# Later modulation steps tied to the end of a weight chunk, the last remainders and pooling sums on one engine, transposes in longer rows

## The chip, the cores and the metric

The kernel runs on one core of one Trainium2 chip. The metric is the device time of one execution in microseconds (us), as the median of several runs; a profiled execution gives the rows of the trace. The profile names the engines PE (TensorE, the matmuls), PEld (its weight loads), DVE (VectorE), ACT (ScalarE), POOL (GpSimd) and SP (SyncE, which here issues the loads of the weights).

## The reference

One decoder layer for 256 new prompt tokens and 8 sequences of 4 new tokens each, so 288 columns in all. Both get the same weights; `c` is a conditioning vector for each sequence.

```python
def decoder_layer(x, c, s0, conv_buf, pool_buf, pos0, w_ada, b_ada, norm1_g, w_in, ..., w_down):
    mod = jax.nn.silu(c) @ w_ada + b_ada
    sh1, sc1, gt1, sh2, sc2, gt2 = jnp.split(mod, 6, axis=-1)
    u = ada_modulate(rms_norm(x, norm1_g), sh1, sc1)
    mix, s_new, conv_new, pool_new = token_mixers(u, conv_buf, s0, pool_buf, pos0, w_in, conv_w, ...)
    x = x + gt1[:, None, :] * mix
    h = ada_modulate(rms_norm(x, norm2_g), sh2, sc2)
    gate, up = jnp.split(h @ w_gate_up, 2, axis=-1)
    x = x + gt2[:, None, :] * ((jax.nn.silu(gate) * up) @ w_down)
    return x, s_new, conv_new, pool_new

def token_mixers(u, ...):
    proj = u @ w_in                        # 2048 -> 9232: q, k, v, z, a, b, xpool, ga, gb
    qkv, conv_new = causal_conv_silu(jnp.concatenate([q, k, v], axis=-1), conv_buf, conv_w)
    ...                                    # gated delta rule over chunks of 64 tokens
    y_p, pool_new = multiscale_pool(xpool, pool_buf, pos0)   # window sums over 2, 4, 8, 16 tokens
    merged = jax.nn.sigmoid(ga) * y_a + jax.nn.sigmoid(gb) * y_b
    return merged @ w_out, s_new, conv_new, pool_new
```

## The kernel before

Every large product goes through `gemm` (L127): a panel of 512 output channels by 288 columns in four PSUM tiles `g` of 128 channels. To keep float32 accuracy, each weight is split into a rounded high part `wh` and a low remainder `wl`, and each 128x128 block is multiplied three times (wh by the high and by the low part of the input, wl by the high part). Weights come in chunks of two blocks of 128 rows: 512 KB, loaded by `load_raw` (L104) through SP's queue into a ring `raw` of 7 slots, cast to `wh` by ACT (L123) and subtracted to `wl` (L124) by DVE or, where `gemm` is told so, by POOL. Four tiles each of `wh` and `wl` hold two chunks. A chunk is 24 matmuls, all on L141.

At the end of each chunk `gemm` calls `fill()` (L146). It counts `every` up and, at each whole number, steps a generator that lays the modulation's products in between: `ada` (L181). A step takes four 512 KB pieces of `w_ada` through the same ring and runs 8 matmuls (L218, tile `ada`; 16 records in the trace); after eight steps four transposes (L225) and an addition (L231) finish 2048 of the modulation's channels. `first_ada` gives those that are needed at once. Three later groups, `later` (M_GT1, M_SC2, M_SH2), are stepped every fifth chunk from the last step of the first product on; `last_ada` (M_GT2) is stepped through the output product and the feed-forward part, with its first two steps' loads ahead.

The first product runs over nine panels (FIRST: q, pooling input, k, pooling input, v, z and three gate panels) in five STEPS of the contraction, so each panel is added into `acc` by DVE at each step after the first (L435). In the last step, four of the nine panels (the odd ones) have their remainders `wl` made by POOL instead of DVE. In that same stretch of time, from about 255 to 345 us, the causal convolution runs on DVE (`conv_evac`, L286, L289, L292), with small copies on POOL (L275 to L281). The pooling branch makes window sums by doubling (`win`, L893): the first of each pair of channel blocks on POOL, the second on DVE; then `yp` (L896 to L900) on DVE.

Three other places transpose on PE: `conv_state_out` (L822, rows of four); the residual input `x` ahead of each of the four panels of the output product (L1011; its tile `xr` takes a slot of a pool of two and is loaded by a DMA that POOL issues, L1008); and `turn` (L1125, tile `pf`) at the end of each panel of the down product.

The tile framework's scheduler puts the instructions of each engine into one order. `tc.high_priority()` makes what is inside go as early as it may, and `tc.issue_after(ins)` puts an instruction behind another one of the same engine in that order.

## Time and profile before

| | |
|---|---|
| median of three runs | 1805.72 us (1804.52 to 1808.49) |
| profiled execution | 1801.66 us |
| its span, first to last instruction | 1799.8 us |
| mean granted TensorE clock | 0.995 |
| PE busy | 1749.2 us, 97% of the span |
| DVE busy | 1001.3 us, 56% |
| ACT busy | 751.0 us, 42% |
| POOL busy | 234.0 us, 13% |

The profiled execution is 1.86 us longer than its span; it lies 4.06 us below the median of the three runs and 2.86 us below the fastest of them. Busy times are means over the whole program; single stretches differ much.

### The profile page before, as it was taken

To read this page: it belongs to the slowest core of one execution; us is meant where nothing else is said; L and a number is where in the kernel's file an instruction comes from. 1 tells how busy PE (TensorE), PEld (TensorE's weight loads), DVE (VectorE), ACT (ScalarE), POOL (GpSimd) and SP (SyncE) were. 2 spreads that over 40 slices of the span, in tenths; PEclk is the share of its full clock that TensorE was granted. 3 is DMA by queue.
4 is the path that set the end of the run, shared out by engine and by line. 5 is a ranking of instruction groups with operands and counts; after the bars stand their busy time and mean duration, and the time that the engine had idled before them with its cause. 6 is when DMAs were issued, how large, how long until landed. Compare 5 with 4: busy or idle time off the path is not lost.

```text
span 1799.8 us, 37784 instructions
## 1 busy us (share of the span) xinstructions
PE 1749.2 (97%) x14772; PEld 1651.6 (92%) x14772; DVE 1001.3 (56%) x2101; ACT 751.0 (42%) x1534; POOL 234.0 (13%) x391
## 2 busy tenths in 40 slices
PE   5999998999999999999999999999999999999997
PEld 3979997888899898899989999999999999999997
DVE  2456569755666676764564444455445445544454
ACT  4523346542344333444444444444334444444333
POOL 1000015420222444211241000000000000000000
PEclk9999999999999999999999999999999999999999
DMA  9988756677577585885647667665555555555542
GB/s 292 316 300 304 234 169 202 213 229 246 187 252 234 189 268 177 271 294 179 218 150 234 211 205 224 188 203 165 164 165 164 168 167 169 154 175 164 162 156 87
DMA packets 227210, 371.23 MB, mean 206 GB/s; under 512 B 18335, under 2 KB 118168, under 8 KB 226608
## 3 DMA queue, kind: packets, MB, share of 16 engines
q1 hardware_dynamic: 223224, 357.02, 61.7%
q0 software_dynamic: 3808, 11.80, 2.1%
q8 instruction: 116, 1.90, 0.4%
q14 instruction: 62, 0.51, 0.1%
HBM read 361.16 MB, written 7.96 MB: 205 GB/s over the span
## 4 chain that ended last, share of the span: by engine, by line
PE 91%; DMA 4%; DVE 2%; issue 1%; ACT 0%; POOL 0%; SPq 0%; DVEq 0%; POOLq 0%; ACTq 0%
PE g L141 81%; PE ada L218 4%; DMA raw<-in_w_ada_dram 3%; DVE wl L124 1%; PE pks L726 1%; DVE cy L286 0%; DMA raw<-in_w_in_dram 0%; PE py L646 0%; PE pp L651 0%; PE pnr L545 0%; PE py L907 0%; DMA xt<-in_x_prompt_dram 0%; PE px L1011 0%; DMA pw<-in_pool_w_dram 0%; DMA dtb<-in_dt_bias_dram 0%
## 5 line engine op out<-in xcount | busy, mean ns | idle before, releaser
L141 PE MATMUL g<-rq,wh 128*128 128x288 f32 x7296 | 1443.2, 298 | 10.6 <-DVE acc L435 6.2
L141 PEld LDWEIGHTS g<-rq,wh 128*128 128x128 f32 x7296 | 1150.8, 188 | 37.2 <-issue 10.9
L141 PE MATMUL g<-rq,wl 128*128 128x288 f32 x3648 | 1014.3, 296 | 0.3 <-POOL wl L124 0.3
L124 DVE TENSOR_TENSOR wl<-raw,wh 128x512 fp32r<-128x512 f32 x910 | 611.7, 702 | 627.0 <-ACT wh L123 606.7
L123 ACT CAST wh<-raw 128x512 fp32r<-128x512 f32 x944 | 545.3, 618 | 821.7 <-PE g L141 742.5
L141 PEld LDWEIGHTS g<-rq,wl 128*128 128x128 f32 x3648 | 664.8, 188 | 4.3 <-issue 1.3
L218 PE MATMUL ada<-raw,cpad 128*32 128x512 f32 (+2 forms) x1152 | 98.5, 474 | 16.0 <-DMA raw<-in_w_ada_dram 16.0
L169 POOL TENSOR_TENSOR ro<-ro,cfix 128x1 f32<-128x1 f32 (+1 forms) x3 | 1.6, 559 | 838.0 <-DVE ro L1150 838.0
L218 PEld LDWEIGHTS ada<-raw,cpad 128*32 128x32 f32 x1152 | 32.9, 115 | 52.8 <-issue 38.1
L435 DVE TENSOR_TENSOR acc<-acc,g 128x288 f32<-128x288 f32 x144 | 61.0, 448 | 23.3 <-PE g L141 23.0
L124 POOL TENSOR_TENSOR wl<-raw,wh 128x512 fp32r<-128x512 f32 x34 | 45.8, 1367 | 51.6 <-ACT wh L123 50.4
L141 PE MATMUL g<-q,wh 128*128 128x288 f32 x256 | 49.4, 294 | 0.0
L286 DVE SCALAR_TENSOR_TENSOR cy<-xc,vb,cy 128x312 f32<-128x312 f32 x72 | 42.5, 610 | 5.6 <-ACT cy L284 4.7
L141 PEld LDWEIGHTS g<-q,wh 128*128 128x128 f32 x256 | 40.3, 189 | 0.0
L141 PE MATMUL g<-q,wl 128*128 128x288 f32 x128 | 35.2, 296 | 0.0
L1099 DVE SCALAR_TENSOR_TENSOR fgg<-fth,fgg 128x288 f32<-128x288 f32 x44 | 20.0, 455 | 14.0 <-ACT fgg L1098 14.0
L973 DVE SCALAR_TENSOR_TENSOR x<-g,mod,x 128x256 f32<-128x256 f32 x48 | 22.9, 478 | 7.0 <-PE g L141 5.9
L1097 ACT ACTIVATE fth<-g 128x288 f32<-128x288 f32 x44 | 18.3, 416 | 13.5 <-PE g L141 13.4
L141 PEld LDWEIGHTS g<-q,wl 128*128 128x128 f32 x128 | 23.2, 188 | 0.0
L659 POOL MEMSET T<- 32x64 f32 x8 | 1.1, 155 | 156.7 <-PE pab L444 148.4
L1104 DVE TENSOR_TENSOR fgg<-fgg,g 128x288 f32<-128x288 f32 x44 | 19.9, 451 | 2.7 <-PE g L141 0.4
L1098 ACT ACTIVATE fgg<-g 128x288 f32<-128x288 f32 x44 | 18.4, 417 | 0.0
(336 smaller groups left out, 976.2 us busy)
## 6 DMA issues: line engine op xcount, KB each, us to landing
raw<-in_w_gate_up_dram SPq DMA_DIRECT2D x352, 256.0 KB, 2.9
raw<-in_w_in_dram SPq DMA_DIRECT2D x144, 512.0 KB, 4.6
raw<-in_w_ada_dram SPq DMA_DIRECT2D x128, 512.0 KB, 5.6
raw<-in_w_down_dram SPq DMA_DIRECT2D x88, 512.0 KB, 4.0
raw<-in_w_ada_dram SPq DMA_DIRECT2D x128, 256.0 KB, 5.5
raw<-in_w_out_dram SPq DMA_DIRECT2D x32, 512.0 KB, 3.9
raw<-in_w_proj_b_dram SPq DMA_DIRECT2D x16, 512.0 KB, 4.5
raw<-in_w_proj_a_dram SPq DMA_DIRECT2D x16, 512.0 KB, 4.6
```

The lines of the kernel that those rows point to most:

```text
L123: act.copy(wh[i], raw[:, i, :])
L124: eng.tensor_tensor(wl[i], raw[:, i, :], wh[i].bitcast(F32), ALU.subtract)
L141: mm = pe.matmul(o, w[i][:, j * P:(j + 1) * P], xs(kbs[c + i])[x], start=c + n == 0, stop=last and n == 3 * KB - 1)
L218: in_turn(pe.matmul(ps[32 * j:32 * j + 32, 0:w], cpad[:, k + i, :], raws[x][:, i, q * w:(q + 1) * w], start=c == 0 and y < 4, stop=c + ste ...
L286: vec.scalar_tensor_tensor(y[:, 0:L], xc[:, m:m + L], vb[:, 24 * m + no:24 * m + no + 1], y[:, 0:L], ALU.mult, ALU.add)
L435: vec.tensor_tensor(a, a, ps, ALU.add)
L726: pe.matmul(pks[NS * i:NS * i + NS, x * P:(x + 1) * P], km[i // 2][:, i % 2, b, :], S[i][:, b, :], start=b == 0, stop=b == NB - 1)
L973: vec.scalar_tensor_tensor(x[:, j, 0:NP], ps[:, 0:NP], mod[:, gate + d, 0:1], x[:, j, 0:NP], ALU.mult, ALU.add)
L1097: act.activation(th, ps, AF.Tanh, scale=0.5)
L1098: act.activation(gg, ps, AF.Copy, scale=0.5)
L1099: vec.scalar_tensor_tensor(gg, th, 1.0, gg, ALU.add, ALU.mult)
L1104: vec.tensor_tensor(gg, gg, ps, ALU.mult)
```

## The change

After each chunk, `gemm` keeps its last matmul in `fill.last`. A step of a late modulation group (16 tiles of output at once, `m == 16`, and not loaded ahead) now stops once more between its loads and its matmuls, and its first matmul is put behind the last matmul of the chunk that was just written out; so a step takes two calls, and `every` is doubled to keep the pace (0.2 to 0.4, and 0.085 to 0.17). In the last step of the first product all `wl` are on DVE, and so are all window sums. The transposes of `conv_state_out`, of `x` and of `turn` are written out together, with the later ones at high priority, and the samples' piece of `xr` takes a slot of the ring `raw`.

```diff
@@ -143,6 +143,7 @@
                 if last:
                     with tc.high_priority():
                         evac(j, o)
+            fill.last = mm
             fill()
         return mm
 
@@ -210,11 +211,14 @@
             yield
         for c in range(0, 16, step * pair):
             loads = early.get(c) or load(c, pool)
+            tied = m == 16 and c not in early
+            if tied:
+                yield
 
             todo = [(k, raws, i, j) for k, raws in reversed(loads) for i in range(step) for j in (2, 3, 0, 1)]
             for y, (k, raws, i, j) in enumerate(todo):
                 x, q = divmod(j, 4 // per)
-                with tc.high_priority() if y else nullcontext():
+                with tc.high_priority() if y else tc.issue_after(fill.last.ins) if tied else nullcontext():
                     in_turn(pe.matmul(ps[32 * j:32 * j + 32, 0:w], cpad[:, k + i, :], raws[x][:, i, q * w:(q + 1) * w],
                                       start=c == 0 and y < 4, stop=c + step * pair == 16 and y + 4 >= len(todo)))
             if c + step * pair < 16:
@@ -241,7 +245,7 @@
 
     class Fill:
 
-        gen, every, n = iter(()), 1.0, 0.0
+        gen, every, n, last = iter(()), 1.0, 0.0, None
 
         def __call__(self):
             self.n += self.every
@@ -425,7 +429,7 @@
 
             more = n + 1 < len(STEPS)
             fill.gen = first_ada(*STEPS[n + 1], st) if more else later
-            fill.every = 4 / (dn // KB * len(FIRST) - 5) if more else 0.2
+            fill.every = 4 / (dn // KB * len(FIRST) - 5) if more else 0.4
             for p, c0 in enumerate(FIRST):
                 def evac(j, ps, n=n, p=p):
                     a = acc[p][:, j, :]
@@ -433,7 +437,7 @@
                         act.copy(a, ps)
                     else:
                         vec.tensor_tensor(a, a, ps, ALU.add)
-                gemm(cols_of(w_in, c0), parts(uh, ul), evac, range(k0, k1), gp if n + p == 0 or not more and p % 2 else vec)
+                gemm(cols_of(w_in, c0), parts(uh, ul), evac, range(k0, k1), gp if n + p == 0 else vec)
                 if p == 1:
                     if n == 0:
                         wab = st.tile([P, 16, 32], F32, name="wab")
@@ -820,11 +824,15 @@
             vec.tensor_tensor(zv, hv(pot), zv, ALU.mult)
 
     def conv_state_out():
+        pls = []
         for p in range(6):
             c0 = 512 * p
-            pl2 = aux("plc")
-            for j in range(4):
-                pe.transpose(pl2[0:27, j * P:(j + 1) * P], cbd[:, 4 * p + j, :], ident)
+            if p % 3 == 0:
+                pls = [aux("plc", i) for i in range(3)]
+                for j in range(12):
+                    with tc.high_priority() if j else nullcontext():
+                        pe.transpose(pls[j // 4][0:27, j % 4 * P:(j % 4 + 1) * P], cbd[:, 4 * p + j, :], ident)
+            pl2 = pls[p % 3]
             ltok = wide("lct")[0:27].rearrange("p h n -> p (h n)")
             act.copy(ltok, pl2[0:27, :])
             dmg(out=t["new_conv_prompt"][0, 0, :, c0:c0 + 512], in_=ltok[0:3, :])
@@ -890,7 +898,7 @@
                     while have < w:
                         nx = pl.tile([P, POOLW], F32, tag="win", name="win", bufs=3)
                         lo = 2 * have - 1
-                        (vec if j else gp).tensor_tensor(nx[:, lo:], s[:, lo:], s[:, lo - have:POOLW - have], ALU.add)
+                        vec.tensor_tensor(nx[:, lo:], s[:, lo:], s[:, lo - have:POOLW - have], ALU.add)
                         s, have = nx, 2 * have
                     yp = pl.tile([P, N], F32, tag="yp", name="yp", bufs=2)
                     vec.scalar_tensor_tensor(yp[:, 0:NP], s[:, 15:XPW], 1.0 / w, src[:, 15:XPW],
@@ -1002,14 +1010,19 @@
     for p in range(4):
         x = fquad(f"x{p}")
         xq.append(x)
+        xrs = []
         for i, (src, n) in enumerate(((t["x_prompt"][0, 0:P], P), (t["x_prompt"][0, P:2 * P], P),
                                       (t["x_sample"].rearrange("b s d -> (b s) d"), NS))):
-            xr = wide("xr")[0:n].rearrange("p h n -> p (h n)")
+            xr = wide("xr").rearrange("p h n -> p (h n)") if i < 2 else load_raw([], kbs=1)[0:n, 0, 0:512]
             dmg(out=xr, in_=src[:, 512 * p:512 * p + 512])
-            px = aux("px")
-            for d in range(4):
-                pe.transpose(px[:, d * n:(d + 1) * n], xr[:, d * P:(d + 1) * P], ident[0:n, 0:n])
-            act.copy(x[:, :, i * P:i * P + n], px[:, 0:4 * n].rearrange("p (d n) -> p d n", n=n))
+            xrs.append((xr, n))
+        pxs = [aux("px", i) for i in range(3)]
+        for y, (i, d) in enumerate((i, d) for i in (2, 1, 0) for d in range(4)):
+            xr, n = xrs[i]
+            with tc.high_priority() if y else nullcontext():
+                pe.transpose(pxs[i][:, d * n:(d + 1) * n], xr[:, d * P:(d + 1) * P], ident[0:n, 0:n])
+        for i, (xr, n) in enumerate(xrs):
+            act.copy(x[:, :, i * P:i * P + n], pxs[i][:, 0:4 * n].rearrange("p (d n) -> p d n", n=n))
 
         def evac(j, ps, p=p, x=x):
             add_gated(x, j, 4 * p + j, ps, M_GT1)
@@ -1037,7 +1050,7 @@
         mm = gemm(cols_of(t["w_out"][0], 512 * p), xs_m, evac, range(16))
     with tc.issue_after(mm.ins):
         next(last_ada)
-    fill.every, fill.n = 0.085, 0
+    fill.every, fill.n = 0.17, 0
 
 
     rn = cst.tile([P, 3], F32, name="rn")
@@ -1123,9 +1136,11 @@
             pfs = [aux("pf", i) for i in range(3)]
 
             def turn(d0, d1, m, p=p, pfs=pfs):
+                for y, (d, i) in enumerate((d, i) for d in reversed(range(d0, d1)) for i in (2, 1, 0)):
+                    t0, n = toks[i]
+                    with tc.high_priority() if y else nullcontext():
+                        pe.transpose(pfs[i][0:n, d * P:(d + 1) * P], xq[p][:, d, t0:t0 + n], ident)
                 for i, (t0, n) in enumerate(toks):
-                    for d in range(d0, d1):
-                        pe.transpose(pfs[i][0:n, d * P:(d + 1) * P], xq[p][:, d, t0:t0 + n], ident)
                     jf = ff.tile([P, 512], F32, tag="jf", name="jf", bufs=2)
                     w = slice(d0 * P, d1 * P)
                     act.activation(jf[0:n, w], pfs[i][0:n, w], AF.Square, accum_out=sso[0:n, i, m:m + 1])
```

What that does to the order of the instructions shows at three places. A row has its number, the line, the operation, the tiles and the shape; in the changed file lines after 146 are 1 to 15 higher. The first place is DVE in the last step of the first product, around the additions into acc_255, the third panel (k). Before:

```order
239 L124 TENSOR_TENSOR wl<-raw,wh 128x512
240 L896 SCALAR_TENSOR_TENSOR yp<-win,xp 128x256
241 L289 SCALAR_TENSOR_TENSOR acc_253<-cth,cy 128x256
242 L292 SCALAR_TENSOR_TENSOR smp<-cth,cy 128x32
243 L900 SCALAR_TENSOR_TENSOR yp<-win,xp 128x32
244 L286 SCALAR_TENSOR_TENSOR cy<-xc,vb,cy 128x312
245 L898 TENSOR_TENSOR yp<-win,icnt 128x15 x2
246 L435 TENSOR_TENSOR acc_255<-acc_255,g_3219 128x288
247 L435 TENSOR_TENSOR acc_255<-acc_255,g_3220 128x288
248 L435 TENSOR_TENSOR acc_255<-acc_255,g_3221 128x288
249 L435 TENSOR_TENSOR acc_255<-acc_255,g_3222 128x288
250 L899 TENSOR_TENSOR yp<-yp,xp 128x15 x2
```

And after:

```order
242 L124 TENSOR_TENSOR wl<-raw,wh 128x512
243 L904 SCALAR_TENSOR_TENSOR yp<-win,xp 128x256
244 L908 SCALAR_TENSOR_TENSOR yp<-win,xp 128x32
245 L124 TENSOR_TENSOR wl<-raw,wh 128x512
246 L290 SCALAR_TENSOR_TENSOR cy<-xc,vb,cy 128x312 x2
247 L906 TENSOR_TENSOR yp<-win,icnt 128x15
248 L439 TENSOR_TENSOR acc_255<-acc_255,g_3228 128x288
249 L439 TENSOR_TENSOR acc_255<-acc_255,g_3229 128x288
250 L906 TENSOR_TENSOR yp<-win,icnt 128x15
251 L439 TENSOR_TENSOR acc_255<-acc_255,g_3230 128x288
252 L439 TENSOR_TENSOR acc_255<-acc_255,g_3231 128x288
```

Before, one `wl` and a run of pooling and convolution rows stand directly ahead of the four additions; after, the `wl` of more chunks (row 245, and row 254 behind) stand here, the sums L901 that fed `yp` have moved ahead of this piece, and the convolution's L293 and L296 of acc_253 have gone behind the additions. POOL's order loses 16 rows of L124 and 10 of L893 over the whole program; DVE's gains them.

The second place is PE in the later panels of w_in, where a modulation step stood 56 matmuls of `g` behind the one before it. Before (row 1895 is the step):

```order
1889 L141 MATMUL g_6391<-rq,wl 128x288
1890 L618 MATMUL pgm<-smp 128x128
1891 L141 MATMUL g_6388<-rq,wh 128x288 x2
1892 L141 MATMUL g_6389<-rq,wh 128x288 x2
1893 L141 MATMUL g_6390<-rq,wh 128x288 x2
1894 L141 MATMUL g_6391<-rq,wh 128x288 x2
1895 L218 MATMUL ada<-raw,cpad 32x512 x8
1896 L141 MATMUL g_6388<-rq,wl 128x288
1897 L141 MATMUL g_6388<-rq,wh 128x288 x2
1898 L141 MATMUL g_6389<-rq,wl 128x288
```

And after, the step that stands nearest to it, at the end of a chunk (g_6388 begins the next panel):

```order
1868 L141 MATMUL g_6017<-rq,wl 128x288
1869 L141 MATMUL g_6018<-rq,wh 128x288 x2
1870 L141 MATMUL g_6018<-rq,wl 128x288
1871 L141 MATMUL g_6018<-rq,wh 128x288 x2
1872 L141 MATMUL g_6018<-rq,wl 128x288
1873 L222 MATMUL ada<-raw,cpad 32x512 x8
1874 L760 MATMUL po<-w,at 128x128 x4
1875 L141 MATMUL g_6388<-rq,wh 128x288 x2
1876 L141 MATMUL g_6388<-rq,wl 128x288
```

Before, the 8 matmuls of a step stood inside a chunk, many of them at distances of 54 to 205 matmuls of `g` from the step before; after, they stand directly behind a chunk, 114 to 126 matmuls of `g` apart. SP's queue keeps its pattern of four pieces of w_ada and five chunks of weights. Counted along both orders, the last three pieces of a step and the first chunk behind them now mostly wait for slots that the step before sets free, and that chunk's first matmul stands 66 to 72 matmuls of `g` behind that step (96 and more for most chunks before).

The third place is PE at the end of the first panel of the down product, where `pf` is made. Before, the first rows of it:

```order
7638 L1128 MATMUL pf<-cfix,x_10696 128x128 x2
7639 L141 MATMUL g_20892<-rq,wh 128x288 x2
7640 L141 MATMUL g_20892<-rq,wl 128x288
7641 L141 MATMUL g_20892<-rq,wh 128x288 x2
7642 L141 MATMUL g_20892<-rq,wl 128x288
7643 L1128 MATMUL pf<-cfix,x_10696 32x128
7644 L1128 MATMUL pf<-cfix,x_10696 128x128 x2
7645 L141 MATMUL g_20891<-rq,wh 128x288 x2
7646 L141 MATMUL g_20892<-rq,wh 128x288
7647 L1128 MATMUL pf<-cfix,x_10696 32x128
7648 L141 MATMUL g_20893<-rq,wh 128x288 x2
```

And after:

```order
7644 L141 MATMUL g_20893<-rq,wh 128x288 x2
7645 L1142 MATMUL pf<-cfix,x_10696 128x128 x8
7646 L141 MATMUL g_20894<-rq,wh 128x288 x2
7647 L141 MATMUL g_20894<-rq,wl 128x288
7648 L141 MATMUL g_20894<-rq,wh 128x288 x2
7649 L141 MATMUL g_20894<-rq,wl 128x288
7650 L1142 MATMUL pf<-cfix,x_10696 32x128 x4
7651 L141 MATMUL g_20891<-rq,wl 128x288
```

The twelve transposes stood in seven rows of one to three among the next panel's matmuls; now they stand in one of eight and one of four. In the order of the x transposes (L1011) the rows stay at four, but those of panels 1 to 3 stand 37 to 51 matmuls of `g` behind the ones that set their slot of `xr` free.

## Rows read from the trace of the kernel before

**Rows 1.** The profile's page: busy time, share of the span, instructions.

```profile
PE 1749.2 (97%) x14772; PEld 1651.6 (92%) x14772; DVE 1001.3 (56%) x2101; ACT 751.0 (42%) x1534; POOL 234.0 (13%) x391
```

**Rows 2.** The chain that ended last: lines' shares; pieces (start, us, what).

```profile
PE g L141 81%; PE ada L218 4%; DMA raw<-in_w_ada_dram 3%; DVE wl L124 1%; PE pks L726 1%; DVE cy L286 0%; DMA raw<-in_w_in_dram 0%; PE py L646 0%; PE pp L651 0%; PE pnr L545 0%; PE py L907 0%; DMA xt<-in_x_prompt_dram 0%; PE px L1011 0%; DMA pw<-in_pool_w_dram 0%; DMA dtb<-in_dt_bias_dram 0%
...
1172.16 506.58 PE g L141 x3816
```

**Rows 3.** What PE waited for, 255 to 345 us: total, times, longest.

```profile
PE g L141 <- DVE acc L435: 5.8, 4, 4.4
...
PE g L141 <- POOL wl L124: 0.3, 1, 0.3
```

**Rows 4.** Timeline of PE: start, us, what, idle before and its releaser.

```profile
284.68 0.50 PE L141 MATMUL g<-rq,wh 128*128 128x288 f32 x2 [4.37 <-DVE acc L435]
```

**Rows 5.** Timeline of DVE around that wait.

```profile
275.59 0.68 DVE L124 TENSOR_TENSOR wl<-raw,wh 128x512 fp32r<-128x512 f32 x1
276.20 0.53 DVE L286 SCALAR_TENSOR_TENSOR cy<-xc,vb,cy 128x312 f32<-128x312 f32 x1
...
280.79 1.48 DVE L289 SCALAR_TENSOR_TENSOR acc<-cth,cy 128x256 f32<-128x256 f32 x1
282.20 1.25 DVE L292 SCALAR_TENSOR_TENSOR smp<-cth,cy 128x32 f32<-128x32 f32 x1
...
286.45 0.58 DVE L893 TENSOR_TENSOR win<-xp 128x422 f32<-128x422 f32 x1
286.95 0.41 DVE L289 SCALAR_TENSOR_TENSOR acc<-cth,cy 128x256 f32<-128x256 f32 x1
287.29 0.21 DVE L292 SCALAR_TENSOR_TENSOR smp<-cth,cy 128x32 f32<-128x32 f32 x1
```

**Rows 6.** Timeline of POOL around it.

```profile
278.76 4.63 POOL L124 TENSOR_TENSOR wl<-raw,wh 128x512 fp32r<-128x512 f32 x3
```

**Rows 7.** Windows: us, busy of PE, PEld, DVE, ACT, POOL, then PEclk, DMA share, GB/s.

```profile
262.00:290.00 28.00, 22.52 (x156) 20.26 (x156) 26.56 (x51) 15.74 (x43) 20.90 (x38) 0.94 0.59 189
285.00:290.00 5.00, 5.00 (x29) 5.00 (x28) 4.93 (x12) 2.65 (x8) 4.02 (x8) 0.66 0.37 111
...
255.00:345.00 90.00, 83.23 (x642) 74.31 (x644) 76.35 (x170) 51.95 (x124) 47.25 (x88) 0.98 0.65 209
```

**Rows 8.** Groups of instructions, 255 to 380 us: count, busy us, mean ns.

```profile
L124 POOL TENSOR_TENSOR wl<-raw,wh 128x512 fp32r<-128x512 f32 x16 | 21.9, 1389 | 19.0 <-ACT wh L123 19.0
L893 POOL TENSOR_TENSOR win<-win 128x420 f32<-128x420 f32 (+2 forms) x6 | 6.9, 1154 | 1.8 <-DVE yp L898 1.5
...
L893 POOL TENSOR_TENSOR win<-xp 128x422 f32<-128x422 f32 x4 | 4.5, 1113 | 10.8 <-ACT xp L859 10.7
```

**Rows 9.** DVE's convolution group, 255 to 345 us.

```profile
L286 DVE SCALAR_TENSOR_TENSOR cy<-xc,vb,cy 128x312 f32<-128x312 f32 x36 | 23.4, 664 | 0.7 <-POOL cbd L280 0.4
```

**Rows 10.** The same group, 345 to 1799 us.

```profile
L286 DVE SCALAR_TENSOR_TENSOR cy<-xc,vb,cy 128x312 f32<-128x312 f32 x36 | 19.2, 556 | 4.9 <-ACT cy L284 4.7
```

**Rows 11.** What PE waited for, 200 to 1799 us.

```profile
PE ada L218 <- DMA raw<-in_w_ada_dram: 1.2, 2, 0.8
```

**Rows 12.** Chain that ended last, from 480 us.

```profile
490.72 9.31 DMA raw<-in_w_ada_dram
...
500.08 1.92 PE ada L218 x16
```

**Rows 13.** Timeline of SP, 480 to 505 us.

```profile
489.27 1.95 SPq L114 DMA_DIRECT2D raw<-in_w_ada_dram  x4
```

**Rows 14.** DMA issues, 480 to 1168 us: count, KB each, median us to landing.

```profile
raw<-in_w_ada_dram SPq DMA_DIRECT2D x88, 512.0 KB, 6.1
```

**Rows 15.** Tile xr (span of the run).

```profile
DMA to landing us min/median/max: 2.2/3.8/6.3
```

**Rows 16.** Chain that ended last, from 834 us.

```profile
839.76 0.44 PE px L1011 x4
```

**Rows 17.** Chain that ended last, from 1715 us.

```profile
1718.34 0.22 PE pf L1128 x2
```

## The prediction, made before the changed kernel ran

> **What bounds the kernel now.** I began with the page: PE is busy for 97% of the span [rows 1]. The chain of work that ended last says the same in another way: 81% of the span is the matmuls of `g`, and its longest piece is 3816 of them in 506.58 us without a gap [rows 2]. That gives the pace of this kernel, 506.58/3816 = 0.13275 us for a matmul, about 3.2 us for a chunk of 24. The number of these matmuls does not change, so the change can only give or take the time in which PE stands still, runs slowly or does something else. I therefore read what PE waited for. In the stretch from 255 to 345 us, which is the last step of the first product, PE waited four times for DVE's additions L435, 5.8 us in all, and once for POOL's `wl`, 0.3 us [rows 3]. One of the four waits is nearly all of it: 4.37 us before 284.68 [rows 4].
>
> Why DVE was late there is seen on its own timeline. The multiply-add L289 takes 0.41 us at 286.95 and took 1.48 us at 280.79; L292 takes 0.21 us and took 1.25 us [rows 5]. In the same microseconds POOL ran three `wl` in a row, from 278.76 to 283.39 [rows 6]. DVE was busy for 26.56 us of the 28 us from 262 to 290 [rows 7]: it was full, and it was full partly of slowed instructions. PE paid twice. After the wait the granted clock was lower for a while: 0.66 as a mean over 285 to 290 us, so partly at the lower of its two levels, 1.2 instead of 2.4 GHz, with 29 matmuls in 5.00 us [rows 7], where 29 x 0.13275 = 3.85 us would do. That is 1.15 us more, and it follows on a stretch in which the engine had stood still for 4.37 us.
>
> **The remainders and the sums on DVE.** Removed from POOL are 16 `wl` of 1389 ns, 21.9 us, and ten sums, 6.9 + 4.5 = 11.4 us [rows 8]. DVE gets them at its own price. The pitch from one start to the next is the honest one, since neighbouring instructions overlap a little: 276.20 - 275.59 = 0.61 us for a `wl` and 286.95 - 286.45 = 0.50 us for a sum [rows 5]. So DVE gains 16 x 0.61 + 10 x 0.50 = 14.8 us of work. What it gets back is the slowing. The 36 multiply-adds L286 in the stretch took 664 ns each [rows 9], the other 36, later, 556 [rows 10]: 36 x 0.108 = 3.9 us. L289 and L292 lost 1.07 and 1.04 us in one place alone [rows 5]. So at least 6.0 us come back on rows that I can price, and at most the 33.3 us of POOL's work. The rest of the 14.8 us must fit into DVE's pauses, which are 90.00 - 76.35 = 13.65 us from 255 to 345 us [rows 7], and it does fit on the whole: 14.8 - 6.0 = 8.8.
>
> Whether it fits at the one place that counts is read from the order. Between the additions to the second and the third panel, DVE now has four `wl`, five L290, three sums, four short `yp` and little else. At 0.61, 0.53 (L286 at 276.20 [rows 5]), 0.50 and some 0.3 us that is 2.4 + 2.7 + 1.5 + 1.2 = 7.8 us, and the four additions follow. PE has 86 matmuls between the same points, 86 x 0.13275 = 11.4 us. So the additions should be ready in time, and the wait of 4.37 us goes, with the 1.15 us of slow clock behind it: **-5.5 us**. The other end on the good side is that every wait of the stretch goes, 5.8 + 0.3 + 1.15 = -7.3. The other end on the bad side is that the wait stays, 0, or that DVE, which has 28.00 - 26.56 = 1.44 us to spare there, becomes later by what the moved `wl` cost; 8 of the 16 and 3 sums stood there, 6.4 us against 1.44 of pause and at least 2.1 of slowing, so +2.9 at worst. I take the middle of the three, since the new order puts the convolution's L293 and L296 behind the additions.
>
> **The tied steps.** They cost no matmul and no load. PE waited twice for a piece of w_ada after 200 us, 1.2 us in all [rows 11]. One of them is in the chain that ended last: the piece took 9.31 us and the step's 16 records began at 500.08 [rows 12]. Its matmuls stood only a few chunks behind the load's issue at 490.72, and the load took 9.31. With 114 to 126 matmuls (15.1 to 16.7 us) between steps that is covered: **-1.2 us**. The other end is 0.
>
> The price stands in the queue behind the step. Three pieces and then one chunk of weights now go out on the slots which a step sets free, and the chunk is wanted 66 to 72 matmuls later. A step takes 1.92 us [rows 12]; the first slot is free some 0.5 us into it, and the chunk must have landed one cast (0.6 us) ahead of its matmul. So it has 1.92 + 72 x 0.13275 - 0.6 = 10.9 us from the step's start. If it lands as most pieces do, 6.1 us after its issue [rows 14], it is there at 1.9 + 6.1 = 8.0 us, and nothing is lost. If it fares as the four pieces that SP issued from 489.27 on [rows 13], the last of which landed at 490.72 + 9.31 = 500.03 [rows 12], four take 10.8 us, and it is there at 0.5 + 10.8 = 11.3 us, 0.4 late with 72 matmuls and 1.2 late with 66. The 24 late steps at some 0.5 us make **0 to +12 us**. I take +1.5, three steps that meet other traffic, because the median piece is 2.9 us early and the one case of 10.8 us was the worst that PE's waits show.
>
> **The transposes.** A row of four on `x` is 0.44 us of the chain [rows 16] and a row of two on `pf` 0.22 [rows 17], so 0.11 us each, in short rows as in long ones. Longer rows neither save nor cost: **0** (0.1 either way). The samples' `xr` no longer takes a slot of the pool of two, so POOL's loads start earlier. But the order puts the prompt's transposes of three panels 37 to 51 matmuls, 4.9 to 6.8 us, behind the release of their slot, and such a load lands after 2.2 to 6.3 us, 3.8 in the middle [rows 15]. Mostly it is there. At worst four rows wait 6.3 - 4.9 = 1.4 us each: 0 to +5.6; I take **+0.7**. The conv state's rows move 24 transposes of unchanged price.
>
> **The sum.** -5.5 - 1.2 + 1.5 + 0 + 0.7 = -4.5 us against the profiled execution, 1801.66 - 4.5 = 1797.2. That execution lies 4.06 us below the median of the three runs, and I add that back: **1801.2 us**. Within 0.2% of 1805.72, that is 3.6 us or 1802.1 to 1809.3, a measurement of this kernel can hardly tell from no change; the forecast lies only just outside.
>
> **The rivals.**
>
> *DVE stays late.* For it speaks that DVE had 1.44 us to spare in the 28 us and gets 6.4 us of work there; against it that the order gives it less ahead of the additions. Then the wait shrinks only by the slowing less the three `wl` that ran beside it, 2.1 - 3 x 0.61 = 0.3 us, and the slow clock stays: -0.3 - 1.2 + 1.5 + 0.7 = +0.7, **1806.4**, the same.
>
> *POOL held DVE for all of its time.* Then DVE gets back much more than the 6 us that I priced, and all the small waits go too: -7.3 instead of -5.5, **1799.4**. The trace has only the slowed rows in POOL's time for it [rows 5, 6], and against it that L286 lost only 108 ns in the mean [rows 9, 10]. The Trainium skill (SBUF — State Buffer, Who interferes with whom) states a rule for this: the two engines share a pair of ports as an exclusive lock, and the loser blocks fully. The trace agrees where L289 and L292 take 1.48 and 1.25 us, but the 36 L286 lost 3.9 us beside POOL's 33.3 us of work, so the lock did not bite all the time. The Trainium skill (Perfetto Trace Analysis, Optimizing Scalar/DVE Operations) says that moving work off a saturated DVE to GpSimd might not help for that reason, which speaks for taking such work back; no run here shows that yet.
>
> *Weights late behind the pieces of w_ada.* For it: the one group of four that a wait shows took 10.8 us. Against it: the median of 6.1. It decides where the chunk lands later than 10.9 us after a step's start. Without the +1.5 the sum is -6.0; 24 steps of 0.5 make it +6.0: 1801.66 + 6.0 + 4.06 = **1811.7**, slower.
>
> *The x transposes wait for their loads.* With +5.6 instead of +0.7 the sum is +0.4: **1806.1**, the same. That the change does not do what it says is not a rival: both orders are there to be read.
>
> **How the numbers follow.** My forecast has 0.41, POOL's full hold 0.14, late DVE 0.25, late weights 0.13, the x transposes 0.07. Faster: all of the full hold and four fifths of the forecast's case, which lies at the bound, 0.14 + 0.33 = 0.47. Slower: the late weights and a few hundredths of late DVE at its worst end (+2.9 with late transposes), 0.16. The rest is the same, 0.37. The likeliest case alone reaches from 1799 to 1803.5. The range goes down to the full hold with the best of the unknown terms (1799.4 - 2.2 - 1.2 = 1796.0) and up to the late DVE at its worst (1806.4 + 2.9 = 1809.3); beyond it lie late weights and little else.
>
> **What would show it.** In the changed profile, PE should wait for L439 in the stretch at most half a microsecond at a time, and no slow clock should follow at 285 us; L290 should take some 560 ns and L293 some 0.4 us there, and DVE should be busy above 85% from 255 to 345 us. No wait for w_ada should be left after 200 us. If weights come late, PE waits for ACT's cast, which waits for raw<-in_w_in or w_proj, once every five chunks. If the loads of `xr` come late, PE waits for them at 820 to 860 us. The prediction is wrong if the wait before the third panel's next matmuls is still above 2 us, or if such waits for casts add up to more than 3 us.

## The result, and the profile after

The changed kernel takes 1814.94 us in the median of five runs (1813.29 to 1815.53), the kernel before 1805.65 in the five beside them: ratio 1.0058, 95% interval 1.0047 to 1.0070. It is slower by 9.3 us, outside the range and on the other side of the forecast. The profiled execution has a span of 1813.2 us against 1799.8 before; some 4 of these 13.4 us are not the change's, since the execution traced before lies 4.06 us below its median.

What was meant to happen to the waits of the first stretch did happen. The waits of PE in the changed kernel, from 255 to 345 us and then from 150 to 1790 (total, times, longest):

```profile
PE pnr L549 <- ACT sq L546: 1.5, 1, 1.5
PE g L141 <- ACT wh L123: 0.9, 2, 0.5
PE g L141 <- DVE smp L296: 0.7, 1, 0.7
...
PE pot L818 <- DVE oo L815: 4.8, 1, 4.8
PE g L141 <- ACT wh L123: 3.2, 6, 0.9
PE g L141 <- ACT rq L1083: 2.3, 1, 2.3
PE g L141 <- DVE ga L967: 2.2, 1, 2.2
```

The waits for DVE's additions, 5.8 us before [rows 3], are gone from the stretch, and no wait for w_ada is left there or later [rows 11]. In their place stand a wait of `pnr` for ACT, six waits for casts (two of them in the stretch), a wait of `pot` for DVE and one of `g` for DVE's `ga`. (The 2.3 us for `rq` are old.) DVE in the stretch, as a window (us, busy of PE, PEld, DVE, ACT, POOL, then granted clock, DMA share, GB/s) and as groups (count, busy us, mean ns):

```profile
255.00:345.00 90.00, 86.84 (x687) 79.06 (x685) 75.79 (x195) 55.10 (x132) 28.56 (x69) 0.96 0.60 196
```

```profile
L124 DVE TENSOR_TENSOR wl<-raw,wh 128x512 fp32r<-128x512 f32 x41 | 27.6, 685 | 7.1 <-ACT wh L123 7.0
L290 DVE SCALAR_TENSOR_TENSOR cy<-xc,vb,cy 128x312 f32<-128x312 f32 x36 | 18.5, 536 | 0.8 <-ACT cy L288 0.7
...
L293 DVE SCALAR_TENSOR_TENSOR acc<-cth,cy 128x256 f32<-128x256 f32 x12 | 5.0, 417 | 0.1
```

Two of these groups before:

```profile
L124 DVE TENSOR_TENSOR wl<-raw,wh 128x512 fp32r<-128x512 f32 x24 | 17.4, 736 | 5.7 <-ACT wh L123 5.2 <-POOL cbd L281 0.5
L289 DVE SCALAR_TENSOR_TENSOR acc<-cth,cy 128x256 f32<-128x256 f32 x12 | 6.7, 561 | 0.3
```

DVE's busy time is 75.79 us where it was 76.35 [rows 7], though it makes 41 `wl` where it made 24: the multiply-adds fell from 664 ns [rows 9] to 536, and what POOL does fell from 47.25 to 28.56 us. What the moved work costs DVE came back from instructions that take less time when POOL does less beside them. The runs below bear this out: the multiply-adds take 538 ns in `b_dve`, which moves this work alone, and 679 in `n_nodve`, which leaves it on POOL. The Trainium skill (Perfetto Trace Analysis, Optimizing Scalar/DVE Operations) says that moving operations between GpSimd and DVE might not help. The trace agrees: with 16 remainders and ten sums taken back, DVE is busy for 997.7 us of the whole program, where it was 1001.3.

Three places show where the time went. First, the wait of `pnr`. The timelines of SP, then of ACT (start, us, what, idle before and its releaser):

```profile
271.88 3.87 SPq L114 DMA_DIRECT2D raw<-in_w_ada_dram  x4
275.79 9.58 SPq L114 DMA_DIRECT2D raw<-in_w_in_dram  x4
```

```profile
285.22 0.62 ACT L123 CAST wh<-raw 128x512 fp32r<-128x512 f32 x1 [1.16 <-DMA raw<-in_w_in_dram]
285.75 1.14 ACT L546 ACTIVATE sq<-acc 128x512 f32<-128x512 f32 x2
```

Four pieces of w_ada went out, and chunks of w_in right behind them. The chain of work of this stretch names one of these loads:

```profile
276.92 8.22 DMA raw<-in_w_in_dram
```

ACT stood before the cast of that chunk, and `sq`, which stands behind the cast on ACT, was what PE waited for. Second, the wait for `ga`, on ACT, DVE and PE:

```profile
800.39 1.14 ACT L123 CAST wh<-raw 128x512 fp32r<-128x512 f32 x2 [6.06 <-DMA raw<-in_w_proj_a_dram]
```

```profile
801.04 0.69 DVE L124 TENSOR_TENSOR wl<-raw,wh 128x512 fp32r<-128x512 f32 x1 [5.92 <-ACT wh L123]
801.65 0.81 DVE L967 SCALAR_TENSOR_TENSOR ga<-ga,g 128x288 f32<-128x288 f32 x2
```

```profile
802.24 0.50 PE L141 MATMUL g<-rq,wh 128*128 128x288 f32 x2 [2.22 <-DVE ga L967]
```

The timeline of SP and the chain of work name the chunk:

```profile
788.98 2.51 SPq L114 DMA_DIRECT2D raw<-in_w_ada_dram  x4
791.59 11.87 SPq L114 DMA_DIRECT2D raw<-in_w_proj_a_dram  x4
```

```profile
791.59 8.70 DMA raw<-in_w_proj_a_dram
```

Here too the chunk directly behind four pieces is late, and what PE waited for is the instruction queued behind its remainder. Third, the longest wait, on POOL and PE:

```profile
651.63 0.89 POOL L945 DMA_DIRECT2D sst<-in_state_delta_dram  x1 [7.07 <-DMA out_dram<-sst]
652.54 0.72 POOL L170 TENSOR_TENSOR m<-m,cfix 128x2 f32<-128x2 f32 x1
```

```profile
655.46 0.66 PE L818 MATMUL pot<-cfix,oo 128*128 128x128 f32 x2 [4.82 <-DVE oo L815]
```

POOL waits 7.07 us for the store of a delta state before it can issue the next reload into that buffer; the small reciprocal root `m`, on which DVE's `oo` and then PE's `pot` wait, stands behind it in POOL's order. Before, the second root stood ahead of the reload next to it, and that reload waited for 0.77 us:

```profile
648.41 0.73 POOL L169 TENSOR_TENSOR m<-m,cfix 128x2 f32<-128x2 f32 x1 [1.33 <-DVE m L808]
649.12 1.29 POOL L780 TENSOR_TENSOR wx<-wr,cm 96x512 fp32r<-96x512 f32 x1
651.17 0.95 POOL L937 DMA_DIRECT2D sst<-in_state_delta_dram  x1 [0.77 <-DMA out_dram<-sst]
```

After each of the three waits the granted clock was lower, partly at 1.2 instead of 2.4 GHz, in windows of 8, 8 and 5 us:

```profile
287.00:295.00 8.00, 8.00 (x41) 8.00 (x41) 6.44 (x16) 3.72 (x11) 1.30 (x8) 0.57 0.33 108
655.00:663.00 8.00, 7.54 (x44) 7.55 (x45) 5.87 (x14) 2.02 (x5) 1.36 (x3) 0.69 0.76 216
802.00:807.00 5.00, 4.76 (x24) 4.79 (x25) 5.00 (x13) 2.10 (x5) 0.53 (x1) 0.66 0.36 110
```

The slower running is the larger part of the loss. The page of the changed kernel has, for the same 14772 instructions [rows 1]:

```profile
PE 1759.5 (97%) x14772; PEld 1658.2 (91%) x14772; DVE 997.7 (55%) x2127; ACT 751.5 (41%) x1534; POOL 205.3 (11%) x365
```

PE is busy for 10.3 us more (1759.5 against 1749.2) and idle for 3.1 us more (span less busy time, 53.7 against 50.6): of the 13.4 us between the two spans, three quarters are PE being busy for longer with the same instructions, and the rest is standing still. The mean granted clock is 0.990, and was 0.995.

### The profile page after: what moved, and what is told of

Its sections match the earlier page's. It is cut to its first block, busy times and chain, and to the rows that moved or that the text cites. A ratio compares the mean times of both kernels' runs of the same rounds, so it can differ in the third digit from the quotient of the medians.

```text
span 1813.2 us, 37744 instructions
## 1 busy us (share of the span) xinstructions
PE 1759.5 (97%) x14772; PEld 1658.2 (91%) x14772; DVE 997.7 (55%) x2127; ACT 751.5 (41%) x1534; POOL 205.3 (11%) x365
## 4 chain that ended last, share of the span: by engine, by line
PE 91%; DMA 6%; DVE 1%; ACT 1%; issue 1%; POOL 0%; SPq 0%; DVEq 0%; ACTq 0%; POOLq 0%
PE g L141 80%; PE ada L222 4%; DMA raw<-in_w_in_dram 1%; DMA raw<-in_w_ada_dram 1%; DMA out_dram<-sst 1%; DMA raw<-in_w_proj_b_dram 1%; PE pks L730 1%; PE py L915 0%; DMA raw<-in_w_proj_a_dram 0%; PE py L650 0%; DVE wl L124 0%; PE pp L655 0%; PE pnr L549 0%; ACT wh L123 0%; DMA xt<-in_x_prompt_dram 0%
## 5 line engine op out<-in xcount | busy, mean ns | idle before, releaser
L124 DVE TENSOR_TENSOR wl<-raw,wh 128x512 fp32r<-128x512 f32 x926 | 618.0, 696 | 636.5 <-ACT wh L123 617.3
L124 POOL TENSOR_TENSOR wl<-raw,wh 128x512 fp32r<-128x512 f32 x18 | 23.9, 1349 | 33.9 <-ACT wh L123 32.8
```

The costliest lines, as they stand in the source:

```text
L124: eng.tensor_tensor(wl[i], raw[:, i, :], wh[i].bitcast(F32), ALU.subtract)
```

## The experiments

The ratios below are those of the runs against runs of the kernel before beside them on the same chip; a difference between two versions is one of medians, which for most pairs were not measured side by side. A trace shows one execution only, and those of `b_tied`, `a_near` and `a_near_root` are the shortest of their runs (1811.70, 1799.70 and 1800.08 us). Theory A says that the tied steps are the loss. Within it, A1 names POOL's order and A2 late weights. Theories B (the longer rows and the ring slot of `xr`) and C (a full DVE) are its rivals.

**Each part alone, and the change without its tied steps.** `b_tied` is the kernel before with the lines of `ada`, `fill.last` and `every` alone; its core:

```diff
+            tied = m == 16 and c not in early
+            if tied:
+                yield
...
-                with tc.high_priority() if y else nullcontext():
+                with tc.high_priority() if y else tc.issue_after(fill.last.ins) if tied else nullcontext():
```

> The kernel before with only the tied modulation steps (and the doubled pace). Theory A (the tied steps are the loss: they move the chunk boundaries, weights come late behind three pieces of w_ada, and POOL's queue puts a reciprocal root behind a state load that waits): the whole loss and the gain of the other parts is missing, so +10 to +16 us against before, with a wait of PE's pot for DVE's oo of 4 to 5 us near 650 us. Theory B (the loss is in the rows: the x transposes and the ring slots taken by the samples' xr): within 3 us of before.

1817.08 us, ratio 1.0063 (1.0042 to 1.0085): the whole loss, as theory A has it. PE's waits for `pot` and for casts, of the sort seen above, are there with this part alone, the one of `pot` shorter than the 4 to 5 us that theory A wanted:

```profile
PE g L141 <- ACT wh L123: 3.0, 4, 1.4
PE pot L818 <- DVE oo L815: 3.0, 1, 3.0
```

`b_dve` takes the `gemm(..., gp if n + p == 0 else vec)` and the `vec` window sums alone.

```diff
-                gemm(..., range(k0, k1), gp if n + p == 0 or not more and p % 2 else vec)
+                gemm(..., range(k0, k1), gp if n + p == 0 else vec)
-                        (vec if j else gp).tensor_tensor(nx[:, lo:], ...)
+                        vec.tensor_tensor(nx[:, lo:], ...)
```

> The kernel before with only the last remainders and all window sums on DVE. Theory A: the wait of 4.4 us before 284.7 us goes and its slow clock with it, -4 to -6 us against before. Theory C (DVE becomes the bound of the stretch and the wait moves): 0 to +3 us.

1804.64 us, ratio 1.0007 (0.9993 to 1.0022): no gain. Theory A, which wanted 4 to 6 us less, missed; the time is in theory C's range, but DVE is not what the trace shows as late. The waits of its PE from 150 to 1799 us:

```profile
PE ada L218 <- DMA raw<-in_w_ada_dram: 6.4, 3, 2.9
...
PE g L141 <- DVE acc L435: 2.3, 2, 1.7
PE pb L607 <- DVE acc L817: 1.7, 1, 1.7
```

DVE's late additions fell from 6.2 to 2.3 us, and the untied steps now waited 6.4 us for pieces of w_ada where they had waited 1.2 [rows 11]. The gain was given back there, at 380, 499 and 964 us.

`b_rows` has the transposes of the three places in longer rows, and the samples' `xr` in the ring.

```diff
-            xr = wide("xr")[0:n].rearrange("p h n -> p (h n)")
+            xr = wide("xr").rearrange("p h n -> p (h n)") if i < 2 else load_raw([], kbs=1)[0:n, 0, 0:512]
...
```

> The kernel before with only the longer transpose rows and the samples' xr in the weights' ring. Theory A: within 2 us of before. Theory B: +3 to +8 us, with a wait of PE's g for DVE's ga or for x loads near 800 us.

1805.53 us, ratio 1.0007 (0.9997 to 1.0016): nothing, as theory A has it. Theory B falls.

`a_notied` is the changed kernel with the lines of `b_tied` taken back.

> The changed kernel with the tied steps taken back (DVE part and rows stay). Theory A: -4 to -6 us against before, no wait of pot for oo near 650 us. Theory B: the wait near 800 us stays and the time is within 2 us of before or above.

1808.77 us, ratio 1.0029 (1.0012 to 1.0046). A miss: theory A wanted 4 to 6 us less than before. Its waits for w_ada come to 5.8 us, much as in `b_dve`; the wait of `pot` is gone. So the DVE part does not keep its gain without tied steps, and by the medians the tied steps account for only 6 of the 9.3 us (1814.94 against 1808.77). The traces say that they account for more. Up to 240 us the engines' orders are the same in the kernel before, in the changed kernel, in `b_dve` and here; yet over the first 150 us the granted clock is 0.94 in this trace and in that of `b_dve`, and 0.98 in the other two. So up to 0.04 x 150 = 6 us of this execution are no part of the change. From 255 to 1790 us, in the kernel before, in the changed kernel and here:

```profile
255.00:1790.00 1535.00, 1520.71 (x12710) 1448.07 (x12708) 865.46 (x1801) 648.00 (x1334) 225.29 (x368) 1.00 0.61 194
255.00:1790.00 1535.00, 1517.19 (x12609) 1441.83 (x12608) 854.85 (x1805) 644.40 (x1319) 196.46 (x341) 0.99 0.60 194
255.00:1790.00 1535.00, 1520.74 (x12695) 1447.01 (x12694) 858.34 (x1812) 647.09 (x1325) 190.69 (x341) 1.00 0.61 195
```

At the 0.13275 us of a matmul in the prediction, the changed kernel is 101 matmuls or some 13 us behind in this stretch, and this one 15 or some 2 us (an estimate, since not all matmuls are alike). The 4 us between its median and that of `b_dve` are hardly apart: the two intervals overlap from 1.0012 to 1.0022.

**POOL's order, and the place of the loads.** `a_root` puts the reloads behind the roots.

```diff
+    r0, r1 = roots[-4], roots[-2]
...
-            dmg(out=s_t, in_=t["state_delta"][0, :, 4 * g + i].rearrange("b k v -> k b v"))
+            with tc.issue_after(r0.ins) if g and i else nullcontext():
+                with tc.issue_after(r1.ins) if g and i else nullcontext():
+                    dmg(out=s_t, in_=t["state_delta"][0, :, 4 * g + i].rearrange("b k v -> k b v"))
```

> The changed kernel, with the second, third and fourth reload of the delta state put behind the two reciprocal roots in POOL's order (an order only, no wait taken away). Theory A1 (the tied steps cost most by POOL's order: a root stood behind a reload that waits 7.07 us for a store): the wait of pot for oo near 655 us and the slow clock behind it go, -6 to -8 us against the changed kernel, so 0 to +4 us against before. Theory A2 (late weights are the loss): -2 us or less against the changed kernel.

1813.73 us, ratio 1.0051 (1.0032 to 1.0070): 1.2 us less than the changed kernel, which these runs can't tell from nothing. A1 falls as the main cause. The wait of `pot` is gone, but its place was taken:

```profile
PE g L141 <- ACT wh L123: 7.9, 9, 3.0
```

The waits for casts rose from 3.2 to 7.9 us, with one of 3.0. I read this so: while PE stood before `pot`, the weights had caught up; with that wait gone they were late themselves.

`a_near` lets three calls pass before a late step's loads are written, so that they come one chunk ahead of its matmuls.

```diff
+            for _ in range(idle):
+                yield
             loads = early.get(c) or load(c, pool)
...
-    later = chain(*(ada(d) for d in (M_GT1, M_SC2, M_SH2)))
+    later = chain(*(ada(d, idle=3) for d in (M_GT1, M_SC2, M_SH2)))
-            fill.every = 4 / (dn // KB * len(FIRST) - 5) if more else 0.4
+            fill.every = 4 / (dn // KB * len(FIRST) - 5) if more else 1.0
```

> The changed kernel, with the loads of each tied step of the first three groups written one chunk ahead of its matmuls instead of two and a half. Counted along the order, the first chunk behind a step's loads has 84 to 96 matmuls in most places where the changed kernel has 66 to 72. Theory A2: PE's waits for casts (3.2 us) and for ga (2.2 us and its slow clock) go, -5 to -8 us against the changed kernel. Theory A1: the wait near 655 us stays as it is, at most -4 us.

1805.34 us, ratio 1.0005 (0.9985 to 1.0024): some 9.6 us less than the changed kernel, and more than the 5 to 8 us that theory A2 wanted. In SP's queue the four pieces of a late step go out one chunk later. The steps' matmuls keep their places, but for one step that stands four matmuls later; the scheduler also moved some rows of POOL, ACT and DVE. PE's waits from 200 to 1790 us:

```profile
PE pot L820 <- DVE oo L817: 3.1, 1, 3.1
...
PE g L141 <- ACT wh L123: 1.2, 4, 0.5
```

The wait for `ga` is gone and those for casts are down to 1.2 us. The wait of `pot` is still there and smaller, and no lower clock follows it (a window of 8 us behind it):

```profile
647.00:655.00 8.00, 8.00 (x65) 8.00 (x66) 6.24 (x15) 3.32 (x7) 3.90 (x6) 1.00 0.88 282
```

`a_near_root` has both edits.

> Both at once. If A1 and A2 each hold a part of the loss, the two gains add: -9 to -14 us against the changed kernel, and -1 to -5 us against before. If waits only move on, within 3 us of the better of the two alone.

1804.80 us, ratio 0.9994 (0.9978 to 1.0010). The two gains do not add: 0.5 us below `a_near` is nothing that these runs tell apart.

`a_split` writes a late step's loads in two halves, two pieces at a time, with `every` at 0.6 and 0.255.

```diff
-            loads = early.get(c) or load(c, pool)
+            loads = [] if tied else early.get(c) or load(c, pool)
+            for i in range(pair if tied else 0):
+                loads += load(c + i * step, pool, 1)
                 yield
...
```

> The changed kernel, with the loads of each tied step written in two halves, earlier still. Counted along the order, chunks behind them have 24 to 48 matmuls instead of 66 to 72. Theory A2 (late weights): many more waits for casts, +10 us or more against the changed kernel. If a chunk needs only what the median load takes (4 to 6 us, 30 to 45 matmuls), within 4 us of the changed kernel.

1813.45 us, ratio 1.0044 (1.0029 to 1.0058): no worse than the changed kernel. Theory A2 wanted 10 us or more above it, and missed here. Its waits for casts are 3.3 us. So the number of matmuls between a slot's release and its use, by which the expectation goes, does not alone say what is late. Smaller groups of loads leave room for a chunk after two pieces instead of after three or four; whether that is the reason, no run shows.

**The loads taken away.** Both kernels leave three of the four pieces of each late step unloaded; the matmuls read the first piece four times, so the later modulation is not computed.

```diff
+                    if m == 16 and raws + loads and pool is None:
+                        raws.append(raws[0] if raws else loads[0][1][0])
+                        continue
                     raws.append(load_raw(srcs, qp if first and k >= 8 else pool, step))
```

> The changed kernel, with three of the four pieces of w_ada in each late step left unloaded (the step's matmuls read the first piece four times, so the later modulation is not the reference's). POOL's order, with the root behind the reload, stays. Theory A2 (weights late behind the pieces is the loss): the waits for casts and for ga go, -9 us or more against the changed kernel, and no more than the kernel before with the same loads left out. Theory A4 (the place of the step at the chunk's end, not the loads, costs time): it stays above the kernel before with the same loads left out, by 5 us or more.

> The kernel before, with the same three of four pieces left unloaded (the later modulation is not the reference's). The wait for DVE's acc of 4.4 us stays; PE waited 1.2 us for pieces and 0.6 us for a cast, so 0 to -3 us against before by all theories.

1797.59 us for the changed one, ratio 0.9945 (0.9923 to 0.9967), and 1800.34 for the kernel before, 0.9971 (0.9955 to 0.9987). The matmuls are those of the changed kernel, the steps keep their places but for six matmuls at one of them, and POOL's second root still stands behind a reload, though some rows of POOL, ACT and DVE changed places. Taking the loads away gives 17.3 us back there (1814.94 - 1797.59) and 4.2 before (1804.52 - 1800.34). Theory A4 falls: without the loads the changed kernel is not the slower of the two (2.7 us less, with intervals that overlap). Its waits for casts, from 200 to 1790 us, and for `pot`:

```profile
PE pot L821 <- DVE oo L818: 2.1, 1, 2.1
...
PE g L141 <- ACT wh L123: 1.0, 2, 0.5
```

The wait of `pot` follows the loads too: POOL waits for that store for 7.07 us in the changed kernel, for 5.65 in `a_near` and for 4.83 here. The edit removes 72 of the 96 loads of those groups and more of the last one, so it bounds what the loads and their place can cost; it does not say which of the two.

How late the weights came can be read for all of them. DMA issues from 480 to 1168 us (count, KB each, median us to landing), in the kernel before [rows 14 has its w_ada, 6.1] and then in the changed kernel:

```profile
raw<-in_w_in_dram SPq DMA_DIRECT2D x54, 512.0 KB, 4.0
...
raw<-in_w_ada_dram SPq DMA_DIRECT2D x88, 512.0 KB, 5.3
raw<-in_w_in_dram SPq DMA_DIRECT2D x54, 512.0 KB, 6.1
```

The pieces land sooner, and the chunks that share the queue with them 2.1 us later. In the same view w_in has 5.8 us in `b_tied` and 6.2 in `a_root`, which lose time as the changed kernel does, 4.0 to 4.2 in `b_dve`, `a_notied` and `b_rows`, 4.6 in `a_near` and 3.9 in `a_noload`. `a_split`, with 4.8, is the exception: it loses time without late chunks in this view.

**What the other parts are worth once the loads are placed near.** Both start from `a_near_root`; `n_norows` has the transposes as before, `n_nodve` the remainders and sums.

> The changed kernel with the loads one chunk ahead and the roots ahead of the reloads, without the longer transpose rows and with the samples' xr in its old pool. If the rows cost or give nothing, within 2 us of the same kernel with the rows (1804.8 us); if the ring slots that xr takes hold weights up, 3 us faster.

> The changed kernel with the loads one chunk ahead and the roots ahead of the reloads, with the last remainders and sums as before on POOL. If moving them to DVE is worth the 5.5 us of the prediction once nothing takes it back, +4 to +6 us against the same kernel with them on DVE (1804.8 us); if it is worth nothing, within 2 us.

1803.48 us, ratio 0.9992 (0.9977 to 1.0008), for the first: the rows are worth nothing here, as alone. 1812.01 us, ratio 1.0031 (1.0018 to 1.0043), for the second: with near loads the DVE part is worth 7.2 us (1812.01 - 1804.80), a little more than expected. What comes back without it is what it was to remove:

```profile
PE g L141 <- DVE acc L443: 5.7, 4, 2.7
```

The second run says one thing more. It stands 7.5 us above the kernel before (1812.01 - 1804.52), though its loads are near and its remainders and sums are as they were. So the tied steps still cost something there, which the DVE part hides in `a_near_root`.

No version that computes the whole layer beats the kernel before by more than its interval.

## Why the prediction was wrong

*The remainders and sums on DVE, -5.5 us.* The mechanism was right. The slowing came back (664 to 536 ns, and L289's 561 to 417), the waits for additions went, and with near loads the part measures -7.2 us. Alone it measures +0.7 us by the medians (-1.3 to +4.0 by the interval), and its trace shows the waits for w_ada grown to 6.4. The slow clock behind 285 us was to go with the wait of 4.37, and the prediction names it as a sign. In `b_dve` it went: from 283 to 297 us the granted clock is 1.00, where it was 0.88 before. In the changed kernel it is 0.76 there, behind the wait of `pnr`. So this part of the gain was taken back on the spot. The stretch before also held a wait of 0.6 us of `pgm` for DVE, which the sum of all waits, -7.3, leaves out. My rival in which DVE stays late did not occur: DVE was busy for some 84% of the 90 us before and after (76.35 and 75.79 us), and PE no longer waited for its additions there.

*The tied steps, -1.2 us for the waits for w_ada.* Right: none is left after 200 us.

*The price in the queue, "0 to +12 us. I take +1.5, three steps that meet other traffic, because the median piece is 2.9 us early".* This is the step that failed. The rival of late weights was the mechanism, with a price worked out at 1811.7 us; the measured time is 1814.94. By the prediction's own sign it is this rival: the waits for casts add up to 3.2 us, more than 3. In place of +1.5, writing the loads one chunk nearer is worth 9.6 us, and the loads taken away give back 17.3 us in the changed kernel and 4.2 in the kernel before, so the loads cost some 13 us more with the change than without it. The mistake has three parts. The median was the wrong number: the chunks in question stand behind the pieces, in the same burst, and the two behind the waits of `pnr` and `ga` took 8.22 and 8.70 us where the median of the pieces was 6.1 [rows 14]; the median of w_in itself rose from 4.0 to 6.1. Of the two delays worked out, 0.4 us with 72 matmuls and 1.2 with 66, the price of 0.5 sits near the smaller. And I priced a late chunk by its own lateness (0.5 us). It costs more than that: what stands behind its cast on ACT or its remainder on DVE is late too (1.5 us of `pnr`, 2.2 of `ga`), and the granted clock is lower after such waits.

*The clock.* I priced it at 1.15 us behind the one wait of 4.37, as a thing that could only go. Behind the waits of 1.5, 4.82 and 2.22 us the granted clock was 0.57 over 8 us, 0.69 over 8 and 0.66 over 5, so the new waits bring the charge three times, and at the first place 41 matmuls in 8.00 us cost 8.00 - 41 x 0.13275 = 2.6 us (an estimate), more than the 1.15 that left. No rival had a price for a new fall of the clock, though PE's longer busy time is three quarters of what the profile lost. A fourth place is the norm ahead of the feed-forward part. There a modulation step runs in 1.85 us before and takes 3.24 in the changed kernel, behind a wait of 1.8 to 1.9 us that both have (before, then after):

```profile
920.28 2.17 PE pn L986 x18
922.45 1.85 PE ada L218 x16
...
930.51 2.17 PE pn L994 x18
932.68 3.24 PE ada L222 x16
```

*The transposes, 0, and `xr`, +0.7.* Nothing speaks against them: +1.6 us by the medians in `b_rows` (-0.5 to +2.9 by the interval) and within 1.3 in `n_norows`, and no wait of the feared kind for the loads of `xr` in the changed kernel.

*What the prediction left out* is POOL's order of roots and reloads, which the diff does not name. The tied steps alone changed it too, and in the changed kernel it made a wait of 4.82 us. Removing that wait alone gave 1.2 us, with longer waits for casts in its trace; so it is no second loss beside the first, but one of two things that were due at the same time.

*What stays open.* `a_split` has the shortest room for a chunk and is not slower than the changed kernel, so a rule by which one could tell from an order alone which burst hurts was not found. That the bursts in SP's queue are what counts rests on `a_near`, on the loads taken away and on the landing times of w_in, not on the count of matmuls. Open too is what the tied steps cost in `n_nodve`: its w_in lands after 4.6 us, as in `a_near`, and what its trace has beside the waits for additions is a granted clock of 0.94 from 255 to 345 us, where the kernel before has 0.98.

## What to carry to other kernels

A load that is written earlier takes its slot of a shared ring earlier, and pays with the load behind it; price the queue by the transfer directly behind the burst, not by the median, and price a late chunk by all that is queued behind its first instruction on every engine. A wait that is removed lets the next resource be late: the DVE part was worth nothing with untied steps, and 7.2 us with tied steps and near loads. A wait in an engine that is otherwise full can cost more behind it than in it: compare busy time and granted clock, not the waits alone. Where a scheduler writes the order, compare all the engines' orders, also at places that the diff does not touch.

## What was not expected of the hardware

That DVE takes over 17 subtractions of some 0.69 us in a stretch of 90 us and is not busy for longer (75.79 us against 76.35). And that a single wait of 1.5 to 4.8 us in an otherwise full PE can be followed by some microseconds at a lower granted clock, whichever engine was late. It need not be: behind the wait of 3.1 us in `a_near`, and behind one of 3.0 in `b_tied`, the granted clock stayed at 1.00, while one of 1.5 was followed by 0.57 over 8 us.
